# Casts of w_out for the second head group, moved behind units of the first products

## The chip, the cores and the metric

The kernel runs on one core of a Trainium2 chip. Its five engines work side by side, each from its own queue in order: TensorE (PE in the profile; its weight loads are PEld), VectorE (DVE), ScalarE (ACT), GpSimd (POOL), and SyncE (SP), which here only issues transfers. The metric is the time of one execution on the device in microseconds (us), lower is better; the median of the runs is compared.

## The reference

An encoder trunk of two layers on 1024 tokens of width 1024, in float32. Each layer computes

```
h = rmsnorm(x, g_pre_mix);  z = h @ w_in;  zf, zq, zk, zv, zm = split(z)
y_f = fourier_mix(zf, w_fourier)                 # 256 wide
y_a = window_attention(rope(zq), rope(zk), zv, sink)   # 8 query heads, 2 key heads, window 128: 512 wide
y_m = memory_attention(zm, keys and values of mem)     # 4 heads on 256 memory rows: 256 wide
y = concat(rmsnorm(y_f), rmsnorm(y_a), rmsnorm(y_m), each with its part of g_grp) @ w_out
x = x + rmsnorm(y, g_post_mix)
h = rmsnorm(x, g_pre_ffn);  gate, up = split(h @ w_ffn_in)
x = x + rmsnorm((silu(gate) * up) @ w_ffn_out, g_post_ffn)
```

The change is about `w_out`, of shape 1024 x 1024: its rows 0 to 255 meet y_f, rows 256 to 767 meet y_a, rows 768 to 1023 meet y_m.

## The kernel before

**Numbers in two parts.** Products of large matrices run in the format float32r. A value is written as a high part, rounded to float32r, and a low part, the rest; a product is then three products, high x high, high x low and low x high (class `Acc`). So each weight tile has to be prepared: ScalarE casts the high part, VectorE (sometimes GpSimd) subtracts it from the value for the low part. For `w_out` the cast also multiplies by the gain `g_grp` of its row (lines 949 and 950, in `load_wout`), where the raw rows come through a ring of three buffers, `raws` (line 948 loads).

**Storage.** Most tiles lie at fixed places of two large arrays, `arena_r` (float32r) and `arena_f` (float32), cut into slots of 256 columns; `Ring` hands out a few places in turn, and a tile may be overwritten once its readers are through. `raws` has slots 0, 2 and 4 of `arena_f`.

**The stage around the change.** Tokens come in 8 tiles of 128. `w_out`'s rows are numbered by blocks k of 128. The stage has these parts, in the order in which they are traced:

- Queries (`q`) and memory attention (`mem_units`), woven with each other, and `fm_load`, which prepares blocks 0, 1, 6 and 7 of `w_out` (Fourier and memory) in the large tiles called `big`.
- `att_units(0)`, the window attention of the first head group: 9 units, one a token tile with the values one unit behind the scores. A unit computes scores on TensorE (line 771), mask and maximum on VectorE (772), exp on ScalarE (784), normalising on GpSimd (795), transposes on TensorE (808), the two parts of the probabilities (162 and 163), and the products with the values (823).
- Woven with these, `fm_units`: 8 units, one for each token tile, that multiply the Fourier and memory columns by their blocks of `w_out`. The text calls them the first products. Each has two column halves; in each half a first group of six matmuls is copied and scaled by ScalarE (line 1006), a second is added by VectorE (1008), and the sum goes to the DRAM tile `pmd`. Preparing a unit's input squares the memory part (960), sums it with TensorE (963) and makes the scale on GpSimd (967).
- `out_load`, one more unit in this weave: it prepares blocks 2 to 5 of `w_out`, which the window attention needs, at slots 32 to 63 of `arena_r`. These are the rows "for the second head group": the products that read them (in `out`, tile name `mo`, with both operands in `arena_r`) run when the second head group of the attention is under way.
- `att_units(1)`, the second head group, with `out`, the residual, the next norm, and the first blocks of the feed-forward network.

**What sets the order.** `weave` merges streams of units by their relative places, which gives the order of tracing. The traced order is only a priority: a planner with its own clock for every engine then lays out each engine's queue, and an instruction that it holds ready may go ahead of others that were traced before it. Casts that only need a load can thus go far ahead of their traced place. `tc.issue_after(ins)` holds them back: what is traced inside it on the engine of `ins` stands behind `ins` in that engine's queue. It adds no wait for `ins` to finish. Transfers that SyncE issues stand in SyncE's queue in planned order; each waits there until the buffer that it writes is free.

In the weave before, the order was: attention unit 0, first products 0, attention 1, first products 1, and so on to attention 6, then `out_load` with all its loads and casts at once, attention 7, first products 6, attention 8, first products 7.

Of the kernel before, what the change touches and what calls it, by code (L numbers as in the profile page):

```python
# [15 lines left out]
AF = mybir.ActivationFunctionType  # L16
ALU = mybir.AluOpType
AX = mybir.AxisListType

P = 128  # L20
# [3 lines left out]
NK = D // P  # L24
# [34 lines left out]
def weave(*streams):  # L59

    order = []
    for si, units in enumerate(streams):
        order += [((i + 0.5) / len(units), si, i, u) for i, u in enumerate(units)]
    for *_, u in sorted(order, key=lambda o: o[:3]):
        u()
# [3 lines left out]
def tile_encoder(ctx: ExitStack, tc: tile.TileContext, T, C, out):  # L69
    nc = tc.nc  # L70
# [11 lines left out]
    def nm(s):  # L82
        uid[0] += 1
        return f"{s}_{uid[0]}"
# [18 lines left out]
    def shaped(ap, shape):  # L103
        names = "abcde"[: len(shape)]
        dims = {c: d for c, d in zip(names, shape)}
        return ap.rearrange(f"p ({' '.join(names)}) -> p {' '.join(names)}", **dims) if len(shape) > 1 else ap

    def at(k, *shape, dt=F32):

        t = arenas[F32R if dt is F32R else F32]  # L110
        if dt is not F32R and k >= 8:
            k, t = (k - 8, flex["t"]) if k < 16 else (k - 8, t)
        o = int(k * 256)
        ap = t[:, o : o + math.prod(shape)]
        return shaped(ap.bitcast(dt) if dt is I32 else ap, shape)

    def big(*shape, dt=F32R):

        return bp.tile([P, *shape], dt, tag="big", name=nm("big"))
# [12 lines left out]
    def run(k, n, step):  # L132
        return Ring(*[k + i * step for i in range(n)])


    raws, junks = run(0, 3, 2), Ring(56)
# [17 lines left out]
    def ps(shape, name="ps", tag="pd"):  # L154
        return psp[tag].tile([P] + list(shape), F32, tag=tag, name=nm(name))

    f32 = lambda ap: ap.bitcast(F32)
# [22 lines left out]
    def cst(*shape):  # L180
# [20 lines left out]
        out=mask[:, 0:P], in_=mask[:, 0:P], pattern=[[1, P]], compare_op=ALU.is_ge,  # L201
# [4 lines left out]
        out=mask[:, 2 * P : 3 * P], in_=mask[:, 2 * P : 3 * P], pattern=[[-1, P]],  # L206
# [3 lines left out]
    ggT = cst(DEPTH * NK)  # L210
# [285 lines left out]
    class Mix:  # L496
# [440 lines left out]

        def load_wout(self, ks, k0=None):

            w = [big(2, D) if k0 is None else at(k0 + 8 * j, 2, D, dt=F32R) for j in range(len(ks))]  # L940
            res = {k: (w[j][:, 0], w[j][:, 1]) for j, k in enumerate(ks)}
            for n in range(2):
                ns = slice(n * 512, n * 512 + 512)
                for k in ks:
                    hi, lo = res[k]
                    g = ggT[:, self.l * NK + k : self.l * NK + k + 1]
                    raw = raws(512)
                    nc.sync.dma_start(raw, T["w_out"][self.l, k * P : (k + 1) * P, ns])
                    nc.scalar.activation(hi[:, ns], raw, AF.Copy, scale=g)
                    nc.vector.scalar_tensor_tensor(  # L950
                        out=lo[:, ns], in0=raw, scalar=g, in1=f32(hi[:, ns]), op0=ALU.mult, op1=ALU.subtract
                    )
            return res

        def group_scale(self, parts, n, ring):

# [24 lines left out]
        def fm_units(self, pmd):  # L981

            st = {}

            def prep(t):
                half, c = divmod(t, 4)
                sl = slice(c * P, c * P + P)
                yf, ym = self.yf[half][:, :, sl], self.ym[half][:, :, sl]
                st[t] = self.split_y((yf, ym), yys), self.group_scale((ym,), MW, sqs)

            def unit(t):
                if t == 0:
                    prep(0)
                (hi, lo), rs = st.pop(t)
                for n in range(2):
                    ns = slice(n * 512, n * 512 + 512)
                    f = pms(512)
                    for gi in range(2):
                        pt = ps([512], "mo")
                        acc = Acc(pt, 2)  # L1000
                        for i in range(2):
                            j = 2 * (1 - gi) + i
                            w = self.wfm[(0, 1, 6, 7)[j]]
                            acc.add(hi[:, j], lo[:, j], w[0][:, ns], w[1][:, ns])
                        if gi == 0:
                            nc.scalar.activation(f, pt, AF.Copy, scale=rs[:, 0:1])
                        else:
                            nc.vector.tensor_tensor(out=f, in0=pt, in1=f, op=ALU.add)
                    nc.scalar.dma_start(pmd[t][:, ns], f)
                if t + 1 < NT:  # L1010
                    prep(t + 1)

            return [lambda t=t: unit(t) for t in range(NT)]

        def out_load(self):
            self.woa = self.load_wout((2, 3, 4, 5), 32)

        def out_gains(self):
            self.gpost = gain(T["g_post_mix"][self.l], at(48, D))
# [332 lines left out]
    mix = Mix(0, hT, mem)  # L1352
# [13 lines left out]
    for l in range(DEPTH):  # L1366
# [6 lines left out]
        mem.load()  # L1373
        weave(mix.mem_units(), q[1:8] + [mix.fm_load] + q[8:])
        fm = mix.fm_units(pmd)
        weave(mix.att_units(0), fm[:6] + [mix.out_load] + fm[6:])
        mix.out_gains()
        xs = x_in if l == 0 else x2d
        hb = Blocks()
# [45 lines left out]
        if l + 1 < DEPTH:  # L1425
            mem = Memory(l + 1, 16, 0, 16, 28, "pT")
            mix = Mix(l + 1, nhT, mem)
# [83 lines left out]
```

## Time and profile before

| | |
|---|---|
| median of 3 runs | 2069.59 us (2065.72 to 2076.48) |
| the profiled execution's own time | 2072.77 us |
| its span, first to last instruction | 2070.9 us |
| mean granted TensorE clock | 0.981 |
| busy: TensorE, VectorE, ScalarE, GpSimd | 2001.5, 1546.8, 1061.7, 714.1 us |
| the stage of the change, layer 0 and layer 1 | about 207 to 294 us and 1227 to 1319 us |

A row of the views of groups and of time has the engine, the line of the kernel, the operation, and output <- inputs by tile names. In brackets stands how long the engine sat idle before it, and what ended that. A row of the view by stage has, for each engine, the busy time in that window and the number of instructions, then the granted TensorE clock as a share of full speed, the share of the transfer engines, and their rate. A row of the waits has who waited, for whom, the total in us, how many times, and the longest.

### The profile page before, as it was taken

The page shows a single profiled execution, that of the slowest core. Times are in us where ns is not written, and L with a number is a line of the kernel's source. Part 1 is how long each engine was busy: PE and PEld are TensorE (multiplying, and loading weights), DVE is VectorE, ACT ScalarE, POOL GpSimd, SP SyncE. Part 2 cuts the span into 40 slices and gives each one's busy share as a digit, 9 for nine tenths or more (in the row PEclk, how much of TensorE's full clock was granted, in tenths as well). Part 3 has the DMA queues.
Part 4 walks back from the last instruction along what each step waited for, and adds up shares of the span by engine and source line. Part 5 has one row for each costly group of instructions (what it writes and reads, how often), then busy time and mean ns, then how long its engine had stood idle before and what let it go on. Part 6 is the DMA issues. An engine that isn't in the chain of part 4 may idle for free.

```text
span 2070.9 us, 28456 instructions
## 1 busy us (share of the span) xinstructions
PE 2001.5 (97%) x9587; PEld 1638.0 (79%) x9587; DVE 1546.8 (75%) x2496; ACT 1061.7 (51%) x2250; POOL 714.1 (34%) x819
## 2 busy tenths in 40 slices
PE   7999999899999999999999989997999999999998
PEld 6877777678888888887888768775888888878886
DVE  5556767888787786768876776579887787778767
ACT  6466777643333333455545677775433333345542
POOL 4354445433343333002423544363342342320002
PEclk9999999899999999999999999998999999999999
DMA  6110222423233233879841122233332233269974
GB/s 212 48 57 31 103 97 102 143 77 107 89 120 97 97 112 104 297 266 332 281 175 39 57 67 93 83 123 121 97 126 95 87 132 97 97 217 342 305 257 155
DMA packets 173634, 286.47 MB, mean 138 GB/s; under 512 B 15496, under 2 KB 73392, under 8 KB 173488
## 3 DMA queue, kind: packets, MB, share of 16 engines
q1 hardware_dynamic: 165424, 265.78, 38.7%
q10 hardware_dynamic: 8064, 18.88, 2.4%
q8 instruction: 75, 1.23, 0.2%
q14 instruction: 71, 0.58, 0.1%
HBM read 218.02 MB, written 66.58 MB: 137 GB/s over the span
## 4 chain that ended last, share of the span: by engine, by line
PE 85%; DVE 4%; DMA 3%; ACT 3%; POOL 3%; issue 2%; SPq 0%; DVEq 0%; POOLq 0%; ACTq 0%
PE fo L1277 19%; PE qz L1142 12%; PE qx L1142 11%; PE qy L1142 11%; PE mo L173 7%; PE qw L1142 6%; PE kvp L173 4%; PE qp L173 4%; PE zT L173 2%; PE pT L808 2%; PE sc L771 1%; DVE arena_r L163 1%; PE av L823 1%; PE av L816 1%; PE mav L916 1%
## 5 line engine op out<-in xcount | busy, mean ns | idle before, releaser
L162 ACT CAST arena_r<-arena_f 128x512 fp32r<-128x512 f32 (+2 forms) x714 | 411.5, 598 | 631.1 <-PE qz L1142 119.8
L163 DVE TENSOR_TENSOR arena_r<-arena_f,arena_r 128x512 fp32r<-128x512 f32 x632 | 476.5, 775 | 138.0 <-ACT arena_r L162 129.7
L1277 PE MATMUL fo<-arena_r 128*128 128x512 f32 x1848 | 424.7, 391 | 5.8 <-ACT arena_r L162 5.8
L1277 PEld LDWEIGHTS fo<-arena_r 128*128 128x128 f32 x1848 | 347.0, 188 | 78.8 <-ACT arena_r L162 4.4
L1142 PE MATMUL qy<-arena_r 128*128 128x512 f32 x1056 | 263.7, 400 | 16.5 <-ACT arena_r L162 11.1
L1142 PEld LDWEIGHTS qy<-arena_r 128*128 128x128 f32 x1056 | 203.3, 193 | 62.6 <-ACT arena_r L162 11.8
L1132 DVE TENSOR_TENSOR arena_f<-arena_f 128x512 f32<-128x512 f32 x220 | 201.9, 924 | 11.5 <-DMA arena_f<-in_w_ffn_in 5.0
L1142 PE MATMUL qz<-arena_r 128*128 128x512 f32 x704 | 199.1, 395 | 2.5 <-ACT arena_r L162 1.9
L1162 POOL TENSOR_TENSOR arena_f<-arena_f 128x512 f32<-128x512 f32 x44 | 71.8, 1633 | 313.7 <-ACT arena_f L1147 313.7
L1142 PEld LDWEIGHTS qz<-arena_r 128*128 128x128 f32 x704 | 134.2, 191 | 31.9 <-ACT arena_r L162 2.6
L1142 PE MATMUL qx<-arena_r 128*128 128x512 f32 x528 | 127.9, 390 | 0.4 <-ACT arena_r L162 0.4
L1142 PE MATMUL qw<-arena_r 128*128 128x512 f32 x528 | 127.3, 389 | 0.0
L1142 PE MATMUL qx<-big,arena_r 128*128 128x512 f32 x528 | 126.8, 389 | 0.0
L1142 PEld LDWEIGHTS qx<-arena_r 128*128 128x128 f32 x528 | 99.2, 188 | 21.7 <-ACT arena_r L162 1.2
L1142 PEld LDWEIGHTS qx<-big,arena_r 128*128 128x128 f32 x528 | 99.1, 188 | 20.6
L1142 PEld LDWEIGHTS qw<-arena_r 128*128 128x128 f32 x528 | 99.1, 188 | 20.6
L1142 PE MATMUL qz<-big,arena_r 128*128 128x512 f32 x352 | 115.2, 389 | 0.0
L221 POOL TENSOR_SCALAR rrsv<-rss 128x1 f32<-128x1 f32 x32 | 17.7, 554 | 259.3 <-ACT arena_f L334 207.3
L173 PE MATMUL qp<-big,arena_r 128*128 128x512 f32 x384 | 99.5, 404 | 2.0 <-POOL big L163 2.0
L173 PE MATMUL mo<-big,arena_r 128*128 128x512 f32 x384 | 101.4, 400 | 0.0
L1194 POOL TENSOR_TENSOR arena_f<-arena_f,flex 128x512 f32<-128x512 f32 x32 | 52.5, 1640 | 139.7 <-DVE arena_f L1174 101.0
L173 PE MATMUL mo<-arena_r 128*128 128x512 f32 x384 | 100.2, 401 | 0.3 <-POOL arena_r L163 0.3
(245 smaller groups left out, 3532.8 us busy)
## 6 DMA issues: line engine op xcount, KB each, us to landing
arena_f<-in_w_ffn_out SPq DMA_DIRECT2D x264, 256.0 KB, 4.6
arena_f<-in_w_ffn_in SPq DMA_DIRECT2D x88, 512.0 KB, 3.6
actd<-arena_f SPq DMA_DIRECT2D x154, 256.0 KB, 3.7
arena_f<-actd SPq DMA_DIRECT2D x154, 256.0 KB, 4.6
arena_f<-in_w_in SPq DMA_DIRECT2D x40, 256.0 KB, 2.8
arena_f<-in_x SPq DMA_DIRECT2D x16, 512.0 KB, 4.8
arena_f<-in_w_out SPq DMA_DIRECT2D x32, 256.0 KB, 2.7
pmd<-arena_f ACTq DMA_DIRECT2D x32, 256.0 KB, 2.0
```

The source lines that it names most:

```text
L162: nc.scalar.copy(hi, src)
L163: return (lo_eng or nc.vector).tensor_tensor(out=lo, in0=src, in1=f32(hi), op=ALU.subtract)
L173: mm(self.dst, a, b, start=self.i == 0, stop=self.i == self.n - 1)
L771: mm(pt, lhs, self.kst[g][i][:, k0 * P : k1 * P], start=i == 0, stop=i == 1)
L808: nc.tensor.transpose(pT[:, h, :], es_[h // 2][:, h % 2, j * P : j * P + P], ident)
L816: mm(av[64 * s : 64 * s + 64, 0 : 2 * P], self.v32[:, k0 + j], rhs, start=j == 0, stop=j == nk - 1)
L823: mm(av, lhs, p_, start=j == 0 and i == 0, stop=j == nk - 1 and i == 1)
L1132: nc.vector.tensor_tensor(out=s, in0=a, in1=b, op=op)
L1142: mm(pt, a, b, start=start and n == 0, stop=n == 11, skip_group_check=not start)
L1162: nc.gpsimd.tensor_tensor(out=self.v, in0=self.v, in1=self.s2, op=ALU.add)
L1194: (G if i in (0, 3) else V).tensor_tensor(out=a[i], in0=c, in1=g[i], op=ALU.mult)
L1277: mm(pt, ab[:, 0, x, sl], ab[:, 1, y], start=new and first and j == 0, stop=last and j == 2, skip_group_check=not new)
```

## The change

`load_wout` is split: `wout_units` returns its eight pieces of work (column half by block, each one load, one cast, one low part) as units, and `load_wout` calls them at once, as before, for blocks 0, 1, 6 and 7. For blocks 2 to 5 the eight units are put into the weave two by two, and each of their casts is traced inside `issue_after` on the last scaled copy (line 1006) traced so far.

```
         def wout_units(self, ks, k0=None, behind=None):
...
+            def unit(n, k):
                 ns = slice(n * 512, n * 512 + 512)
...
+                raw = raws(512)
+                nc.sync.dma_start(raw, T["w_out"][self.l, k * P : (k + 1) * P, ns])
+                with tc.issue_after(self.scaled.ins) if behind else ExitStack():
                     nc.scalar.activation(hi[:, ns], raw, AF.Copy, scale=g)
+                nc.vector.scalar_tensor_tensor(
+                    out=lo[:, ns], in0=raw, scalar=g, in1=f32(hi[:, ns]), op0=ALU.mult, op1=ALU.subtract
+                )
+
+            return res, [lambda n=n, k=k: unit(n, k) for n in range(2) for k in ks]
...
-                            nc.scalar.activation(f, pt, AF.Copy, scale=rs[:, 0:1])
+                            self.scaled = nc.scalar.activation(f, pt, AF.Copy, scale=rs[:, 0:1])
...
         def out_load(self):
-            self.woa = self.load_wout((2, 3, 4, 5), 32)
+            self.woa, units = self.wout_units((2, 3, 4, 5), 32, True)
+            return units
...
-        weave(mix.att_units(0), fm[:6] + [mix.out_load] + fm[6:])
+        ld = mix.out_load()
+        weave(mix.att_units(0), fm[:2] + [u for i in range(4) for u in ld[2 * i : 2 * i + 2] + fm[2 + i : 3 + i]] + fm[6:])
```

The second stream of the weave has 16 pieces now instead of 9, so the first products' places among the attention units change too. The traced order is, with A for an attention unit, F for a unit of the first products and W for a piece of `w_out`, all counted from 0: F0 A0 F1 W0 A1 W1 A2 F2 W2 A3 W3 F3 A4 W4 W5 A5 F4 W6 A6 W7 A7 F5 F6 A8 F7. W0 and W1 are pinned behind F1's second scaled copy, W2 and W3 behind F2's, W4 and W5 behind F3's, W6 and W7 behind F4's. The low parts on VectorE and the loads on SyncE are not pinned. The data, the number of instructions and the places in memory are the same.

More of the change, by code (lines that the diff above doesn't have):

```diff
@@ L938, in load_wout, with wout_units @@
         def load_wout(self, ks, k0=None):
+            res, units = self.wout_units(ks, k0)
+            for u in units:
+                u()
+            return res
+        def wout_units(self, ks, k0=None, behind=None):
             w = [big(2, D) if k0 is None else at(k0 + 8 * j, 2, D, dt=F32R) for j in range(len(ks))]
             res = {k: (w[j][:, 0], w[j][:, 1]) for j, k in enumerate(ks)}
-            for n in range(2):
+            def unit(n, k):
                 ns = slice(n * 512, n * 512 + 512)
[L944 to L948, printed above, removed]
+                hi, lo = res[k]
+                g = ggT[:, self.l * NK + k : self.l * NK + k + 1]
+                raw = raws(512)
+                nc.sync.dma_start(raw, T["w_out"][self.l, k * P : (k + 1) * P, ns])
+                with tc.issue_after(self.scaled.ins) if behind else ExitStack():
                     nc.scalar.activation(hi[:, ns], raw, AF.Copy, scale=g)
[L950 to L953, printed above, removed]
+                nc.vector.scalar_tensor_tensor(
+                    out=lo[:, ns], in0=raw, scalar=g, in1=f32(hi[:, ns]), op0=ALU.mult, op1=ALU.subtract
+                )
+            return res, [lambda n=n, k=k: unit(n, k) for n in range(2) for k in ks]
         def group_scale(self, parts, n, ring):
```

## The prediction

> **What bounds the kernel now.** I read the page first, then the busy times by stage around the moved casts, then who TensorE waited for in those stages, and then the queues of ScalarE and VectorE in order of time.
>
> From the page:
>
> ```profile
> span 2070.9 us, 28456 instructions
> PE 2001.5 (97%) x9587; PEld 1638.0 (79%) x9587; DVE 1546.8 (75%) x2496; ACT 1061.7 (51%) x2250; POOL 714.1 (34%) x819
> ```
>
> TensorE is the bound: 2070.9 - 2001.5 = 69.4 us of its span are idle, over the whole kernel. A change that moves casts can take only some of that, or add to it.
>
> The moved casts are line 949 with an arena_r output, 8 in each layer, each followed by its low part, line 950, on VectorE. The instructions of line 949 (x, ns min/median/max, first and last start):
>
> ```profile
> L949 ACT ACTIVATE arena_r<-arena_f,const x16: 707/722/755, 207.9 to 1243.3; 128x512 fp32r<-128x512 f32 x16
> ```
>
> All 16 lie in two stretches, which I call the heads of the stage. The next view gives busy time for each head and then for the rest of its stage, in layer 0 and layer 1, and for a window at the end.
>
> ```profile
> core 0: us, PE busy (x) PEld busy (x) DVE busy (x) ACT busy (x) POOL busy (x), PEclk, DMA share, GB/s
> 207.00:226.00 19.00, 15.74 (x76) 9.74 (x75) 15.64 (x49) 16.96 (x45) 8.08 (x15) 1.00 0.35 114
> 226.00:294.00 68.00, 68.00 (x364) 57.57 (x365) 43.74 (x129) 47.03 (x121) 27.94 (x48) 1.00 0.31 106
> 1227.00:1245.00 18.00, 14.52 (x79) 9.25 (x77) 16.63 (x46) 17.12 (x47) 10.51 (x18) 1.00 0.34 111
> 1245.00:1319.00 74.00, 74.00 (x396) 62.05 (x393) 49.57 (x154) 52.40 (x141) 29.94 (x52) 1.00 0.30 102
> ```
>
> ```profile
> 300.00:310.00 10.00, 9.00 (x55) 6.16 (x53) 6.09 (x27) 10.00 (x32) 5.49 (x10) 1.00 0.00 0
> ```
>
> In the heads TensorE is idle 19 - 15.74 = 3.26 us and 18 - 14.52 = 3.48 us, together 6.74 us, while ScalarE is busy 0.89 and 0.95 of the time and VectorE 0.82 and 0.92. In the rest of the stage TensorE has no idle time that the view shows, and ScalarE is at 47.03/68 = 0.69 and 52.40/74 = 0.71. So the casts sit where ScalarE and VectorE bind, and go to where TensorE binds. That is the case for the change; its size is what the 6.74 us allow.
>
> What TensorE waited for in the two heads (total us, times, longest):
>
> ```profile
> PE mav L916 <- ACT arena_f L908: 1.7, 2, 1.4
> PE sc L771 <- DVE rmax L772: 0.8, 3, 0.3
> PE pT L808 <- POOL arena_f L795: 0.4, 1, 0.4
> ```
>
> ```profile
> PE mpT L906 <- POOL arena_f L896: 1.7, 3, 0.8
> PE sc L771 <- DVE rmax L772: 1.2, 2, 0.8
> PE mav L916 <- ACT arena_f L908: 0.5, 1, 0.5
> ```
>
> No row names a cast: line 949 delays what TensorE waits for only by standing in front of it in an engine's queue. ScalarE's queue in order of time (start, us):
>
> ```profile
> 207.90 0.72 ACT L949 ACTIVATE arena_r<-arena_f,const 128x512 fp32r<-128x512 f32 x1
> 208.53 0.40 ACT L960 ACTIVATE arena_f<-arena_f 128x256 f32<-128x256 f32 x1
> 208.83 1.05 ACT L908 COPY arena_f<-mpT 128x512 f32<-128x512 f32 x2
> ...
> 217.02 0.72 ACT L949 ACTIVATE arena_r<-arena_f,const 128x512 fp32r<-128x512 f32 x1 [1.13 <-DMA arena_f<-in_w_out]
> 217.65 0.49 ACT L784 ACTIVATE arena_f<-arena_f,nmx 128x256 f32<-128x256 f32 x1
> ...
> 1227.30 0.72 ACT L949 ACTIVATE arena_r<-arena_f,const 128x512 fp32r<-128x512 f32 x1
> 1227.91 0.57 ACT L417 CAST arena_r<-qT 64x512 fp32r<-64x512 f32 x1
> 1228.38 1.07 ACT L908 COPY arena_f<-mpT 128x512 f32<-128x512 f32 x2
> ```
>
> And VectorE's:
>
> ```profile
> 213.15 1.05 DVE L950 SCALAR_TENSOR_TENSOR arena_r<-arena_f,const,arena_r 128x512 fp32r<-128x512 f32 x1
> 214.13 0.41 DVE L772 CUSTOM_DVE_ANT_0 arena_f<-sc,const 128x256 f32<-128x256 f32 x1
> ...
> 216.27 0.15 DVE L778 SCALAR_TENSOR_TENSOR nmx<-rmax,const 128x4 f32<-128x4 f32 x1
> ...
> 1235.30 0.75 DVE L950 SCALAR_TENSOR_TENSOR arena_r<-arena_f,const,arena_r 128x512 fp32r<-128x512 f32 x1
> 1235.97 0.42 DVE L772 CUSTOM_DVE_ANT_0 arena_f<-sc,const 128x256 f32<-128x256 f32 x1
> ```
>
> One cast holds ScalarE for 208.53 - 207.90 = 0.63 us, one low part holds VectorE for 1235.97 - 1235.30 = 0.67. The worst is at 217.02: the cast waits 1.13 us for its own load, and the exps (line 784) stand behind it although their bias was ready at 216.27 + 0.15 = 216.42. They start 217.65 - 216.42 = 1.23 us late.
>
> **The change part by part.** No instruction is added or removed: 8 loads, 8 casts and 8 low parts in each layer, as before. Moved are: the casts (pinned), the low parts (behind their casts), the loads from the fourth on (three raw buffers), and the traced places of the first products' units among the attention units.
>
> Taken from the heads. A wait can lose at most the one cast in front of it.
> - 1.4 us before mav, layer 0: the cast at 207.90 delays line 908 by 0.63. Gain 0.63.
> - 0.4 before pT, layer 0: its probabilities come from the exps that were 1.23 late. Gain 0.4.
> - sc, layer 0, 0.8 in three: the low part at 213.15 holds the mask and maximum (line 772) for 0.98 us; one wait, 0.3.
> - mav, layer 1, 0.5: the cast at 1227.30. Gain 0.5, all of it.
> - sc, layer 1, the longest of 0.8: the low part at 1235.30. Gain 0.67.
> - mpT, layer 1, 1.7 in three: this chain goes through VectorE, where a low part can cost between 0 and 0.67; I take 0.3.
>
> Sum 0.63 + 0.4 + 0.3 + 0.5 + 0.67 + 0.3 = 2.8 us. The bounds are 0 (each wait's next releaser is as late) and 6.74 (all idle time of the heads).
>
> Added behind the first products. 16 casts at 0.63 are 10.1 us of ScalarE, 5 us in each layer; its share there becomes (47.03 + 5.0)/68 = 0.77 and (52.40 + 5.0)/74 = 0.78. 16 low parts at 0.67 make VectorE (43.74 + 5.4)/68 = 0.72. What hides them is TensorE's own queue, which has no idle time in either window. If that cover were gone, every cast would show: 10.1 us, the upper bound; below nothing it cannot go, as nothing there waits on these casts. I take the end near 0, 0.5 us, since with ScalarE at 0.69 to 0.71 TensorE's idle time is nothing.
>
> Is the last cast early enough? It goes behind the fifth unit's second scaled copy, the tenth line 1006 of the layer; the first reader is the second head group's product:
>
> ```profile
> 263.80 0.69 ACT L1006 ACTIVATE arena_f<-mo,grs 128x512 f32<-128x512 f32 x1
> ...
> 1287.37 0.69 ACT L1006 ACTIVATE arena_f<-mo,grs 128x512 f32<-128x512 f32 x1
> ```
>
> ```profile
> L173 PE MATMUL mo<-arena_r x384: 387/393/501, 293.9 to 1407.1; 128*128 128x512 f32 x192
> ```
>
> ```profile
> 1319.03 1.55 PE L173 MATMUL mo<-arena_r 128*128 128x512 f32 x6
> ```
>
> 293.9 - 263.8 = 30 us and 1319.0 - 1287.4 = 32 us of cover. Cost 0; if it were gone, the output product of the first token tile would wait, and TensorE has only attention to fill with.
>
> The loads. A fourth load can go out when the first low part has read its buffer, a unit ahead of its cast (eight units in 68 us, so 8.5 us); it lands in
>
> ```profile
> DMA to landing us min/median/max: 2.5/2.7/3.8
> ```
>
> so no cast should wait. On SyncE's queue these loads now pass, or are passed by, the early loads of the residual stage; one of those (the projected rows of tile 2) goes into raw buffers 0 and 2 and must now wait for the last casts. It is read long after 300 us. Cost 0. The same holds for POOL's sum of the values (line 834), which overwrites the third raw buffer and is read only from the second head group on.
>
> [...] At 213.15 the low part took 1.05 instead of 0.75 while this ran:
>
> ```profile
> 211.82 1.85 POOL L896 TENSOR_SCALAR arena_f<-arena_f,rden 128x256 f32<-128x256 f32 x4 [4.30 <-DVE rden L894]
> ```
>
> [...]
>
> **The sum.** The profiled execution took 2072.77 us, its span 2070.9 and 1.9 around it. 2072.77 - 2.8 + 0.5 = 2070.5. The median of the runs is 2069.59, 3.2 below this execution; on that scale 2069.59 - 2.3 = 2067.3, so **2067**.
>
> **Rivals.**
>
> 1. The heads clear completely. Units 0 and 1 of the first products are now traced ahead of attention units 0 and 1, so the planner may also fill the heads with them. All 6.74 us go: 2063. For: ScalarE and VectorE are the only thing late there. Against: the remaining waits run through chains of three engines (maximum, exp, normalising, transposes) that the casts do not lengthen. A larger form: weight loads take only 9.74/19 = 0.51 and 9.25/18 = 0.51 of the heads, against 57.57/68 = 0.85 in the rest. Were 0.85 possible, the heads would need (9.74 + 9.25)/0.85 = 22.3 us instead of 37: 14.7 us of room, 2055. Against that form:
>
> ```profile
> 209.45 1.07 PE L916 MATMUL mav<-arena_f 128*64 128x512 f32 x2 [1.43 <-ACT arena_f L908]
> ```
>
> Two products of the memory values take 1.07 us here, so few loads belong to much of the work. [...]
>
> 2. Nothing to see: the big tiles' casts and the softmax chains keep the heads as late as they are. Casts hidden before, hidden after: 2069.6.
>
> 3. Slower: the end of the stage. Of the 16 traced pieces, units 4 and 5 of the first products now come later among the attention units (4 behind attention unit 5 instead of 4, 5 behind 7 instead of 5, all counted from 0), so more of the first products falls into 300 to 310 us, where ScalarE is at 10.00 of 10. A unit brings two scaled copies of 0.69 and about three instructions of line 960's size (0.40): 2.6 us. Up to two units in each layer make 10.4 us: 2080; it is slower than before from the point where one unit falls there, since 2 x 2.6 is more than the 2.8 gained. For: the full window. Against: TensorE is idle there for only 1 us, and more first products there would also fill it.
>
> 4. Slower: a moved load stands on SyncE's queue behind a load that waits for something else, its cast then holds ScalarE with the exps behind it, as at 217.02. One landing of 2.7 for each of three pairs in two layers is 16 us: 2086. Against: the loads have a unit's time in hand.
>
> **How the numbers follow.** I give the forecast 0.46, rival 2 0.15, rival 1 at 2063 0.13 and in the direction of 2055 0.08, rival 3 0.12, rival 4 0.06. Faster or slower means by over 0.5%, about what a measurement of this kernel can tell: below 2059.2 or above 2079.9. Faster: 0.08 and some of 2063, with the runs' own spread (2065.72 to 2076.48), 0.13. Slower: rival 4 and about half of rival 3, 0.12. Within: 0.75. The range takes in rival 1 at 2063 with the spread below it and rival 3 at its price: 2057 to 2079. The likeliest case's own range is 2062 to 2072.
>
> **What would show it.** Right: no line 949 with arena_r output before the second unit's scaled copies (line 1006); ScalarE below 0.8 in the head; mav's wait of 1.4 us near 0.8; TensorE still without idle time to 290 us. Wrong: idle TensorE between 226 and 310 us released by line 949, 784 or 162 (rival 3 if it lies behind 290), or line 949 waiting for a load of w_out (rival 4). A difference that arises after 390 us, at the start of the feed-forward network, would be a new order by the planner that none of these steps holds.

## The result and the profile after

| | before | after |
|---|---|---|
| median (12 runs each) | 2071.40 us (2065.72 to 2076.58) | 2066.66 us (2061.78 to 2072.07) |
| profiled execution's own time | 2072.77 us | 2072.07 us |
| its span, granted clock | 2070.9 us, 0.981 | 2070.3 us, 0.986 |

The ratio of after to before is 0.9969, with an interval of [0.9955, 0.9983]: faster by 0.3%, which is some 6 us (the medians of the table lie 4.7 us apart), and within 0.5%. The forecast was 2.3 us. The profiled execution of after is the slowest of its 12; a second profile of the same kernel (run e1 below) had a span of 2059.0 us, so where the two disagree both are shown.

From the page of after:

```profile
PE 1994.9 (96%) x9587; PEld 1634.8 (79%) x9587; DVE 1551.5 (75%) x2496; ACT 1059.5 (51%) x2250; POOL 715.3 (35%) x819
```

TensorE is busy 2001.5 - 1994.9 = 6.6 us less with the same 9587 matmul instructions, at a higher mean clock. That is the first sign that the gain isn't idle time taken out.

**The casts went where the change sends them.** The group of the moved casts in after (line 957 there; the scaled copy they are pinned behind is line 1015), and ScalarE's queue around the first pair:

```profile
L957 ACT ACTIVATE arena_r<-arena_f,const x16: 708/711/714, 229.8 to 1282.3; 128x512 fp32r<-128x512 f32 x16
```

```profile
229.20 0.68 ACT L1015 ACTIVATE arena_f<-mo,grs 128x512 f32<-128x512 f32 x1
229.78 1.32 ACT L957 ACTIVATE arena_r<-arena_f,const 128x512 fp32r<-128x512 f32 x2
```

The pair stands right behind a scaled copy, without the 1.13 us in which a cast of before waited for its load.

**The stage by busy time.** The same parts of the stage in after (head, rest of the first products, products of the second head group, for each layer):

```profile
202.00:221.00 19.00, 17.63 (x96) 12.09 (x94) 13.92 (x51) 15.73 (x48) 9.08 (x19) 1.00 0.13 45
221.00:292.00 71.00, 69.39 (x369) 58.80 (x368) 51.76 (x152) 53.62 (x138) 30.87 (x49) 1.00 0.37 123
292.00:381.00 89.00, 87.49 (x514) 67.33 (x513) 61.88 (x125) 64.10 (x161) 48.80 (x76) 1.00 0.34 116
1223.00:1241.00 18.00, 16.24 (x85) 9.95 (x84) 12.27 (x40) 15.12 (x49) 8.25 (x17) 1.00 0.14 45
1241.00:1319.00 78.00, 76.14 (x409) 64.43 (x408) 59.58 (x176) 60.44 (x163) 34.75 (x57) 1.00 0.33 112
1319.00:1407.00 88.00, 86.57 (x501) 65.66 (x500) 60.40 (x120) 59.17 (x150) 45.65 (x72) 1.00 0.33 117
```

And the two parts of before that the prediction didn't show:

```profile
294.00:390.00 96.00, 93.24 (x538) 70.13 (x536) 68.36 (x150) 69.87 (x182) 51.75 (x80) 1.00 0.33 114
1319.00:1407.00 88.00, 87.80 (x519) 68.14 (x518) 60.23 (x131) 65.89 (x170) 46.61 (x77) 1.00 0.33 113
```

TensorE's idle time (window less busy), both layers together:

| part | before | after |
|---|---|---|
| heads | 6.74 us | 1.37 + 1.76 = 3.13 us |
| rest of the first products | 0 | 1.61 + 1.86 = 3.47 us |
| second head group | 2.76 + 0.20 = 2.96 us | 1.51 + 1.43 = 2.94 us |
| sum | 9.70 us | 9.54 us |

The heads are relieved by 3.6 us, and 3.5 us of new idle time stand behind the first products. The runs e2 and e3 below tell apart what the moved casts and the new order of the units did here. TensorE's waits there in after, layer 0 from 221 us and layer 1 from 1241 us:

```profile
PE mo L173 <- DVE flex L845: 1.1, 1, 1.1
PE sc L771 <- DVE rmax L772: 0.4, 1, 0.4
```

```profile
PE av L823 <- DVE arena_r L163: 1.5, 1, 1.5
```

These waits all name VectorE, which also makes the moved low parts. The stage as a whole has not less idle time than it had.

**The start of the feed-forward network.** The gain is found behind the stage. The first 60 us after the last product of `out`, layer 0, first of before, then of after, in steps of 10 us:

```profile
390.00:400.00 10.00, 3.44 (x12) 2.28 (x12) 9.56 (x16) 5.34 (x10) 4.04 (x4) 0.62 0.35 121
400.00:410.00 10.00, 9.32 (x23) 6.83 (x24) 9.28 (x14) 4.66 (x9) 3.35 (x2) 0.53 0.33 103
410.00:420.00 10.00, 6.98 (x33) 5.11 (x31) 9.17 (x15) 5.92 (x12) 2.94 (x2) 0.98 0.30 106
420.00:430.00 10.00, 8.54 (x19) 5.81 (x20) 10.00 (x18) 5.38 (x11) 0.00 (x0) 0.51 0.01 2
```

```profile
381.00:391.00 10.00, 3.99 (x15) 2.65 (x14) 9.21 (x14) 5.42 (x11) 7.34 (x5) 0.67 0.39 125
391.00:401.00 10.00, 6.96 (x23) 5.21 (x23) 9.19 (x14) 5.69 (x10) 3.12 (x3) 0.84 0.61 191
401.00:411.00 10.00, 7.14 (x33) 5.08 (x32) 9.96 (x16) 5.76 (x11) 0.00 (x0) 0.97 0.18 52
411.00:421.00 10.00, 10.00 (x45) 8.02 (x44) 8.81 (x16) 7.00 (x14) 4.95 (x2) 1.00 0.01 2
```

The first three rows of both are nearly alike in matmul instructions started (12, 23, 33 and 15, 23, 33; products and transposes together, in the text "products"). In the fourth, before starts 19 at a granted clock of 0.51, and after 45 at 1.00: that is the difference. What TensorE had in its queue there, first before (its fourth row begins at 420 us; the last line shown are the next 22 `qz` products), then after:

```profile
413.54 3.02 PE L1142 MATMUL qy<-arena_r 128*128 128x512 f32 x12 [0.68 <-ACT arena_f L1147]
416.40 0.60 PE L1071 MATMUL hTp<-const,arena_f 128*128 128x128 f32 x4
418.12 0.66 PE L1071 MATMUL hTp<-const,arena_f 128*128 128x128 f32 x4 [1.12 <-ACT big L1072]
420.49 1.22 PE L1142 MATMUL qz<-arena_r 128*128 128x512 f32 x2 [1.71 <-ACT arena_r L162]
423.90 8.10 PE L1142 MATMUL qz<-arena_r 128*128 128x512 f32 x22 [0.54 <-DVE arena_r L163]
```

```profile
402.28 0.63 PE L1081 MATMUL hTp<-const,arena_f 128*128 128x128 f32 x4 [0.64 <-DVE arena_f L305]
403.39 2.57 PE L1152 MATMUL qy<-arena_r 128*128 128x512 f32 x10 [0.48 <-DVE arena_r L163]
405.81 0.60 PE L1081 MATMUL hTp<-const,arena_f 128*128 128x128 f32 x4
408.14 3.01 PE L1152 MATMUL qy<-arena_r 128*128 128x512 f32 x12 [1.74 <-ACT arena_f L1157]
```

`hTp` are the transposes of the normalised tokens (two halves of four for the last tile), `qy` and `qz` the first products of the feed-forward network. In before all 48 `qy` products of the tiles that are ready stand ahead of the last tile's transposes, and behind these nothing is left to do but wait for their copies and casts. In after the planner set the transposes behind 26 and 36 of the 48, so that 22 `qy` products fill the gaps. The change touches none of these instructions; their places are the planner's.

### The profile page after: what moved, and what is told of

It is laid out like the page before. It is cut to its first block, busy times and chain, and to the rows that moved or that the text cites. A ratio compares the mean times of both kernels' runs of the same rounds, so it can differ in the third digit from the quotient of the medians.

```text
span 2070.3 us, 28479 instructions
## 1 busy us (share of the span) xinstructions
PE 1994.9 (96%) x9587; PEld 1634.8 (79%) x9587; DVE 1551.5 (75%) x2496; ACT 1059.5 (51%) x2250; POOL 715.3 (35%) x819
## 4 chain that ended last, share of the span: by engine, by line
PE 79%; DVE 5%; DMA 5%; POOL 4%; ACT 4%; issue 3%; SPq 0%; DVEq 0%; POOLq 0%; ACTq 0%
PE fo L1287 16%; PE qz L1152 11%; PE qx L1152 11%; PE qy L1152 11%; PE mo L173 6%; PE qw L1152 5%; PE qp L173 4%; PE kvp L173 4%; PE zT L173 2%; DVE arena_r L163 2%; PE pT L808 1%; PE sc L771 1%; DMA arena_f<-in_w_ffn_out 1%; DMA arena_f<-actd 1%; POOL arena_f L795 1%
## 5 line engine op out<-in xcount | busy, mean ns | idle before, releaser
L1287 PE MATMUL fo<-arena_r 128*128 128x512 f32 x1848 | 429.1, 394 | 13.0 <-ACT arena_r L162 10.9
L1152 PE MATMUL qz<-arena_r 128*128 128x512 f32 x704 | 195.5, 389 | 0.0
L163 POOL TENSOR_TENSOR arena_r<-arena_f,arena_r 128x256 fp32r<-128x256 f32 (+2 forms) x82 | 68.1, 835 | 97.0 <-ACT arena_r L162 72.8
```

The lines of the kernel that those rows point to most:

```text
L163: return (lo_eng or nc.vector).tensor_tensor(out=lo, in0=src, in1=f32(hi), op=ALU.subtract)
L1152: mm(pt, a, b, start=start and n == 0, stop=n == 11, skip_group_check=not start)
L1287: mm(pt, ab[:, 0, x, sl], ab[:, 1, y], start=new and first and j == 0, stop=last and j == 2, skip_group_check=not new)
```

## The experiments

In the expectations, H is the prediction's reading (the heads of the stage carry the gain, the new place costs next to nothing), and S the theory formed on the comparison above: the gain arises at the start of the feed-forward network, from how many `qy` products stand ahead of the last transposes.

To read all runs alike, each execution is cut at the same instructions: "stage" runs from the first product of the memory scores (`ms`; in layer 1 from the last product of the queries, `qp`) to the last product of `out` (`mo`), and "start" from there to the last `qy`. For layer 0 of after, they come from these rows (first and last start):

```profile
L884 PE MATMUL ms<-flex,arena_r x64: 274/282/385, 138.6 to 201.2; 128*128 128x256 f32 x64
L173 PE MATMUL mo<-arena_r x192: 387/393/504, 295.6 to 381.4; 128*128 128x512 f32 x192
L1152 PE MATMUL qy<-arena_r x528: 387/389/796, 387.8 to 810.8; 128*128 128x512 f32 x176
```

The stage is 381.4 - 138.6 = 242.8 us and the start 810.8 - 381.4 = 429.4 us. "Ahead" is the number of `qy` products ahead of each half of the last transposes (one number where both halves stand together), layer 0 then layer 1; "products" is the number of matmul instructions, transposes among them, that TensorE began in the first 60 us after the last `mo`.

| run | ratio to before [interval] | ahead | products | stage 0 | start 0 | stage 1 | start 1 | sum |
|---|---|---|---|---|---|---|---|---|
| before | 1 | 48; 26 | 172; 199 | 247.6 | 435.9 | 192.4 | 431.8 | 1307.7 |
| e9, before again | 1.0007 [0.9991, 1.0024] | 48; 26 | 172; 207 | 250.5 | 435.8 | 192.6 | 429.8 | 1308.7 |
| after | 0.9969 [0.9955, 0.9983] | 26/36; 26/36 | 200; 206 | 242.8 | 429.4 | 196.0 | 430.1 | 1298.3 |
| e1, after again | 0.9951 [0.9933, 0.9969] | 26/36; 26/36 | 202; 204 | 242.8 | 428.9 | 195.8 | 430.5 | 1298.0 |
| e2, pin only | 0.9940 [0.9920, 0.9961] | 26; 26 | 208; 212 | 246.0 | 427.6 | 195.2 | 427.2 | 1296.0 |
| e11, pin only again | 0.9937 [0.9919, 0.9955] | 26; 26 | 197; 213 | 242.0 | 430.1 | 193.6 | 427.0 | 1292.7 |
| e3, order only | 0.9981 [0.9966, 0.9997] | 36/48; 26 | 189; 220 | 245.2 | 431.7 | 202.5 | 426.9 | 1306.3 |
| e4, no casts | 1.0023 [1.0009, 1.0037] | 48; 48 | 171; 171 | 246.5 | 436.1 | 195.5 | 436.1 | 1314.2 |
| e5, before, transposes early | 1.0020 [1.0007, 1.0034] | 24; 24 | 194; 192 | 240.2 | 431.7 | 202.6 | 431.3 | 1305.8 |
| e6, after, transposes late | 1.0017 [1.0004, 1.0029] | 48; 48 | 174; 188 | 245.2 | 435.3 | 195.9 | 434.3 | 1310.7 |
| e7, casts twice | 1.0011 [0.9995, 1.0026] | 36/48; 26 | 179; 206 | 245.2 | 434.0 | 201.1 | 429.9 | 1310.2 |
| e8, pin only, transposes early | 1.0001 [0.9986, 1.0016] | 24; 24 | 196; 195 | 240.2 | 431.2 | 198.3 | 432.7 | 1302.4 |
| e10, before, 12 products held | 0.9981 [0.9967, 0.9995] | 36; 26 | 192; 204 | 250.5 | 431.2 | 193.3 | 430.4 | 1305.4 |

Two profiles of one kernel agree within 0.6 us in the start of layer 0 (e2 and e11: 2.5 us), 2.0 us in the start of layer 1, and 3 to 4 us in the stage of layer 0. Smaller differences than these are not read from the lengths. For all runs but e5 and e8, whose stage begins some 5 to 11 us later than the others', the sums go with the ratios to within 4 us. All starts with 48 products ahead of both halves took 434.3 to 436.1 us, and all others 426.9 to 434.0. Among these the number doesn't order them: with 26 ahead they took 426.9 to 431.8 us.

**The stage without the clock's part.** Most of what one kernel's stage varies by is the granted clock. In some executions it is at half for a stretch of the stage, in others of the same queues it is not, as at the stage's start in e9 (after and e1 have 1.00 there):

```profile
138.00:145.00 7.00, 6.14 (x18) 5.14 (x19) 6.84 (x13) 3.96 (x8) 4.50 (x6) 0.51 0.02 4
```

As an estimate from the clock of 0.51, half of TensorE's busy time in such stretches is lost, here 6.14/2 = 3.1 us, and 4.7 in the whole stage with a second such stretch at 353 us (0.98 over the window from 291 to 388 us). The next table takes that off each stage. Beside it stands TensorE's idle time in two parts, both layers together: A from the first of the first products (`mo` from `big`) to the first `mo` of the second head group (the heads and what follows them), B from there to the last `mo`. For before, A is 91.00 - 87.74 us of the window from 202.9 to 293.9 us and 97.70 - 93.18 us of the one from 1221.3 to 1319.0.

| run | stage 0 less the loss | stage 1 less the loss | sum | idle A | idle B |
|---|---|---|---|---|---|
| before; e9 | 246.0; 245.8 | 192.4; 192.6 | 438.4; 438.4 | 7.8; 8.1 | 3.0; 2.8 |
| after; e1 | 242.8; 242.8 | 196.0; 195.8 | 438.8; 438.6 | 7.4; 7.6 | 2.9; 3.0 |
| e2; e11 (pin only) | 241.2; 242.0 | 193.6; 193.6 | 434.8; 435.6 | 4.5; 4.5 | 4.1; 4.0 |
| e3 (order only) | 243.5 | 196.0 | 439.5 | 9.4 | 2.5 |
| e4 (no casts) | 243.4 | 195.5 | 438.9 | 5.2 | 5.0 |
| e7 (casts twice) | 243.6 | 201.1 | 444.7 | 9.0 | 4.1 |

By this measure two profiles of one kernel agree within 0.8 us. (e6 and e10 have the stage's queues of after and of before; e5 and e8 are left out, as their queues differ from the start on.) The change took some 3 us from stage 0 and added as much to stage 1.

**e1, the changed kernel again** (no edit), for a second profile of it.

> The changed kernel once more, for a second profile. In the first profile of it the heads' idle TensorE fell from 6.7 us to 3.1, but 3.5 us of idle time appeared behind the first products, and the feed-forward start of layer 0 ran at a granted clock of 0.98 instead of 0.80. Theory H (the heads): ratio 0.997, and the place of the gain is the time from the first product mo to the last one, shorter by 2 to 4 us in each layer. Theory S (the start of the feed-forward network, where the planner's order of the last transposes has moved): ratio 0.997 too, but the stage as long as before and 6 us won between the last mo and the last qy of layer 0. If the clock of 0.98 was chance, this profile shows about 0.80 there.

Ratio 0.9951, and all four parts within 0.5 us of after's. Against the mean of before and e9, e1 has 249.1 - 242.8 = 6.3 us less in stage 0 (that part alone varies by 3 us), 3.3 us more in stage 1, 6.9 us less in start 0, and 0.3 us less in start 1. The two stages together are 3.0 us shorter, but without the clock's part they are as long as before (438.6 against 438.4), so this is chance; start 0 is the part that stands clear of it.

**e2 and e11, the pin without the new order.** The traced order of attention units and first products is that of before; only the casts move. The weave, against that of before (the pin itself is the change's):

```
-        weave(mix.att_units(0), fm[:6] + [mix.out_load] + fm[6:])
+        ld = mix.out_load()
+        pair = [lambda i=i: [u() for u in (fm[i], ld[2 * i - 2], ld[2 * i - 1])] for i in range(1, 5)]
+        weave(mix.att_units(0), fm[:1] + pair + [fm[5], lambda: None] + fm[6:])
```

> The casts are pinned two by two behind the same units as in the change, but attention units and first products keep the traced order of before. Theory H: all of the gain is here, 0.996 to 0.998. Theory S (the new weave order and what the planner makes of the feed-forward start): 1.000, with the feed-forward start of layer 0 between. Either: no cast with an arena_r output in the heads.

> The kernel that only pins, once more, as the candidate to beat both: 0.994 to 0.996 by its first timing. Theory S: 428 and 427 us from the last mo to the last qy, as in its first profile.

0.9940 and 0.9937: at least as fast as the whole change, and the fastest version of the study (median 2059.96 us in e11). So the new traced order isn't needed for the gain. Its starts took 854.8 and 857.1 us (before 867.7, 865.6). Its stages took 441.2 and 435.6 us (before 440.0, 443.1); without the clock's part that is some 3 to 4 us less than before. TensorE in the head of layer 0, behind it, and the same in layer 1, up to the second head group, in e2:

```profile
205.00:224.00 19.00, 17.28 (x88) 11.97 (x87) 13.53 (x49) 14.00 (x40) 9.06 (x18) 1.00 0.19 60
224.00:290.80 66.80, 66.64 (x360) 56.69 (x359) 49.74 (x138) 52.44 (x137) 26.74 (x43) 1.00 0.38 127
1220.00:1238.00 18.00, 16.20 (x81) 9.94 (x81) 12.56 (x40) 14.85 (x47) 7.42 (x16) 1.00 0.15 47
1238.00:1313.70 75.70, 75.62 (x415) 64.25 (x414) 56.79 (x172) 58.39 (x153) 32.11 (x52) 1.00 0.35 115
```

The heads' idle time is 1.72 + 1.80 = 3.5 us, as in after, but behind the first products it is 0.16 + 0.08 = 0.24 us, although the 16 casts stand there too and ScalarE is at 0.79 and 0.77. With the second head group (1 us more than before) the stage has 8.6 us of idle time (8.5 in e11), 2.2 to 2.4 less than the 10.8 and 10.9 of before and e9. That is the reading H, and nearly the forecast's own size, but for the pin without the new order.

**e3, the new order without the pin.** The weave of after, with `wout_units((2, 3, 4, 5), 32)`, so that no cast is held back.

> The eight units in the new weave order, but nothing pinned: the planner puts the casts into the heads as before. Theory H: no gain, 1.000, with ScalarE at 0.9 and 3 us of idle TensorE in each head. Theory S: the gain is here, 0.997, with the last transposes of the stage among the first qy products as in the changed kernel.

0.9981. The two stages took 447.7 us, 9.1 more than e1's 438.6. Most of that is no price of the casts' place: in the head of layer 1 this one profile had half the clock,

```profile
1227.00:1241.00 14.00, 13.39 (x47) 10.78 (x46) 9.38 (x32) 11.53 (x34) 8.00 (x12) 0.51 0.21 73
```

and without the clock's part the stages are 439.5 against 438.6 us. In idle time A the pin is worth 1.8 to 2.0 us in the new order (9.4 to 7.4 and 7.6) and 3.3 to 3.6 in the old (7.8 and 8.1 to 4.5). The new order by itself adds 1.3 to 1.6 us (7.8 and 8.1 to 9.4), and does not relieve the heads. The starts are 7 to 9 us shorter than before's (two profiles).

**e4, no casts at all.** Before, with the 16 loads, casts and low parts of blocks 2 to 5 left out; the products read whatever lies at those slots.

```
-            self.woa = self.load_wout((2, 3, 4, 5), 32)
+            w = [at(32 + 8 * j, 2, D, dt=F32R) for j in range(4)]
+            self.woa = {2 + j: (w[j][:, 0], w[j][:, 1]) for j in range(4)}
```

> Traced order of before, with the 16 loads, casts and low parts of blocks 2 to 5 of w_out left out (the products then read what is left in those slots, so the output is not the reference's). This is the most that any place for the casts can give. Theory H: 0.995 to 0.997, since the heads are relieved and nothing is added later; by the forecast 2.8 us in the heads, 6.7 at most. Theory S: 1.000 or any small difference that the order of the feed-forward start makes, whose PE order is that of before here.

Slower, 1.0023, with less work. The two heads, by busy time in e4:

```profile
204.00:223.00 19.00, 16.66 (x86) 11.07 (x86) 11.90 (x44) 13.02 (x39) 9.14 (x18) 1.00 0.04 15
1222.00:1240.00 18.00, 15.34 (x86) 10.43 (x85) 14.69 (x41) 15.94 (x49) 9.27 (x18) 1.00 0.05 18
```

TensorE is still idle 2.34 + 2.66 = 5.0 us there: without any cast only 1.7 of the 6.74 us go. By idle time A, which doesn't depend on where a head's window is cut, it is 2.6 to 2.9 us, of which 2.0 to 2.2 come back in B. The stages together took 442.0 us, between before's 440.0 and 443.1. Here the planner laid out the stage anew without the casts, and nothing of the relief is left in its length; the time lost is at the start of layer 1, where all 48 products now stand ahead of the transposes as in layer 0 (431.8 to 436.1 us).

**e7, the price of the new place.** After, with each of the 16 pinned casts and its low part made twice.

```
+                for _ in range(2 if behind else 1):
+                    with tc.issue_after(self.scaled.ins) if behind else ExitStack():
+                        nc.scalar.activation(hi[:, ns], raw, AF.Copy, scale=g)
+                    nc.vector.scalar_tensor_tensor(
+                        out=lo[:, ns], in0=raw, scalar=g, in1=f32(hi[:, ns]), op0=ALU.mult, op1=ALU.subtract
+                    )
```

> The changed kernel with each of the 16 moved casts and its low part made twice, at the new place. The forecast's price of the new place was 0.5 us for 16 casts: by it this differs from the changed kernel by under 1 us in the stretch from the first mo to the last mo. If every cast shows there, that stretch is 5 us longer in each layer. The start of the feed-forward network has 36 and 48 qy ahead of the last transposes in layer 0 and 26 in layer 1, so by theory S it adds 3 us in layer 0 and takes 3 in layer 1.

The stages took 2.4 and 5.3 us more than e1's, 7.7 us for 16 more casts with their low parts; without the clock's part it is some 6 us, 0.4 us each, of 0.63 on ScalarE and 0.67 on VectorE. This is a rough price from one profile, nearly all of it in layer 1, and TensorE's order in the stage is no longer that of after (from 234 us on), so it is not the casts' alone. It is the price of one more cast in the new order, where one stands already; the first 16 cost 0.24 us of idle time in the old order (e2). The other part of the slowdown is start 0 (434.0), where the order fell back to 36 and 48.

**e6, after with the last transposes late.** One edge that adds no wait: the last tile's transposes stand behind all 48 `qy` products, as in layer 0 of before. Up to the start of the feed-forward network all queues are those of after.

```
+                    lastqy[0] = mm(pt, a, b, start=start and n == 0, stop=n == 11, skip_group_check=not start)
...
+                with tc.issue_after(lastqy[0].ins) if i == NT + 3 else ExitStack():
+                    hb.tile(hs.pop(i - 4), i - 4)
```

> The changed kernel, with the last tile's transposes held behind all 48 qy products on TensorE's queue in both layers, which is where the kernel before has them in layer 0. Theory S: the stretch from the last mo to the last qy rises from 429 us to about 436 in layer 0 and from 430 to about 436 in layer 1, the gain is gone: 0.999 to 1.002. Theory H: the heads stay relieved and the gain stays, 0.996.

1.0017: the whole gain is gone, and more. Start 0 took 435.3 us, 5.9 more than after's and 0.6 less than before's; start 1 434.3, 4.2 more than after's. In the first 60 us of start 0 its clock was between those of the two (0.86; before 0.77, after 0.91), and TensorE was idle 3 us longer than in either (14.9 us): here the late order cost idle time as well as clock.

**e10, before with 12 products held.** The other direction: in before, the first of the last 12 `qy` products gets an edge without a wait that puts it behind the last transposes. All queues of layer 0 are those of before until there.

```
+                if i == NT + 3:
+                    tc.add_manual_dep(
+                        held[0].ins, lastT[0].ins.name,
+                        mybir.DependencyInfo(mybir.DependencyClass.NoSync, mybir.DependencyReason.DATA),
+                        reason="held",
+                    )
```

> The kernel before with one edge more: in TensorE's queue the up half's product 4 stands behind the last token tile's transposes. All queues are those of before up to the start of layer 0's feed-forward network; there 36 qy products stand ahead of the last transposes instead of 48, and VectorE's queue follows. Layer 1 has 26 already and keeps them. Casts are where they were. Theory S: the stretch from the last mo to the last qy of layer 0 falls from 436 us to about 432, as in the run with the new order only, nothing else moves: 0.998. Theory H: 1.000.

0.9981 [0.9967, 0.9995], with start 0 at 431.2 us, 4.7 less than before, and stage 0 at 250.5 as in e9. TensorE's queue in e10:

```profile
417.36 0.63 PE L1071 MATMUL hTp<-const,arena_f 128*128 128x128 f32 x4 [2.42 <-DVE arena_f L305]
418.67 1.11 PE L1071 MATMUL hTp<-const,arena_f 128*128 128x128 f32 x4 [0.68 <-ACT big L1072]
419.43 4.10 PE L1143 MATMUL qy<-arena_r 128*128 128x512 f32 x12
424.28 5.15 PE L1143 MATMUL qz<-arena_r 128*128 128x512 f32 x22
```

The 12 products stand where before had its waits, and the 22 `qz` products then take 5.15 us, where the 22 of before at 423.90 took 8.10. This is the cleanest test of S: the stage has its old casts and its old order, and a good part of the gain of the change is there.

**e5 and e8, the transposes earlier by the traced order.** Two groups of 12 `qy` products (`uq`, the up half, with their load) are traced one step later, behind the last tile's transposes, in before (e5) and in the pin-only version (e8), so that 24 `qy` products stand ahead of the transposes.

```
+            if i == NT + 3:
```

> The kernel before, casts untouched, with one edit elsewhere: at the start of the feed-forward network the up half's products 2 and 4 are traced behind the last token tile's transposes. On TensorE's queue 24 qy products then stand ahead of the last transposes in both layers, instead of 48 in layer 0 and 26 in layer 1. Theory S (the place of the last tile's chain in the queues sets the start): the stretch from the last mo to the last qy falls in layer 0 from 436 us to about 427, and in layer 1 from 432 by 2 to 5; ratio 0.994 to 0.996, about the whole gain of the change without moving a cast. Theory H (the heads): 1.000, since the heads are as before.

> Casts pinned with the unit order of before, as in the run that pinned only, and the up half's products 2 and 4 traced behind the last transposes, as in the run that moved them alone. Theory S: 24 qy ahead of the last transposes in both layers where the pinned kernel has 26, so about the same as that: 0.993 to 0.995. If the two edits' gains added up, as theory H and S side by side would have it, 0.990.

Both missed: 1.0020 and 1.0001. The 24 came out in both layers of both runs, and the starts took 431.2 to 432.7 us: better than with 48, but not the 427 that was expected of fewer ahead. And the new traced order made the planner lay out every queue anew from the very start of the kernel (TensorE's differs within the first 15 us): the stage began at 147.0 and 148.6 us instead of 142.1, and stage 1 of e5 took 202.6. They change too much to test one thing by their whole time; e10 with its single edge does that.

**e9, before again** (no edit), for a second profile.

> The kernel before once more, for a second profile of it: ratio 1.000. If its first profile was a usual one, the last mo to the last qy takes 436 us in layer 0 and 432 in layer 1, and the two stages 248 us (first memory score to last mo, layer 0) and 192 us (last query product to last mo, layer 1). Its first memory score came 3.5 us later than in the kernels with pinned casts, whose queues are the same up to there; if that was chance it comes at 139 us here.

1.0007, an interval that holds 1. Start 0 is 435.8 us and 172 products again, so the slow start is a property of the order, not of one execution. It also shows how much stage 0 varies with the same queues (247.6 and 250.5, nearly all of it the clock's part), and that the 3.5 us by which after entered the stage earlier (138.6 against 142.1) are chance: e9 entered it at 137.5.

## Why the prediction was right, and where it was wrong

The time was right by its number: forecast 2.3 us faster, measured 0.3% (some 6 us), and "within 0.5%" held. For the change as it was made this is luck: the stage that was to carry the gain carried none of it, and what came arose elsewhere. The mechanism, casts out of the heads, was right for the pin without the new order (e2 and e11: 2.2 to 2.4 us of idle time less in the stage). The step that failed is the new order of the units. The sum has terms for the casts alone and puts the order at nothing; it appears only among the rivals. It costs TensorE some 3 us of idle time up to the second head group and some 2 in the whole stage, and all but some 0.4 us of the relief is gone with that (10.3 and 10.6 us in after and e1, 8.6 and 8.5 in e2 and e11).

- "Taken from the heads", 2.8 us: measured 3.6 (6.74 to 3.13). TensorE's waits in the heads of after, layer 0 and layer 1:

```profile
PE mav L916 <- ACT arena_f L908: 1.0, 2, 0.6
PE mpT L906 <- POOL arena_f L896: 0.2, 1, 0.2
```

```profile
PE mpT L906 <- POOL arena_f L896: 1.2, 2, 0.8
PE sc L771 <- DVE rmax L772: 0.3, 1, 0.3
PE mav L916 <- ACT arena_f L908: 0.2, 1, 0.2
```

  mav's longest in layer 0 went from 1.4 us to 0.6 (forecast near 0.8), sc's total in layer 1 from 1.2 to 0.3 and mav's from 0.5 to 0.2. The pin does this without the new order too (e2: 6.74 to 3.5), so it can be put down to the casts' place. What rival 1 named, units 0 and 1 of the first products traced ahead of the attention's, doesn't do it: with the new order alone (e3) idle time A is 9.4 us, where before and e9 have 7.8 and 8.1. That the heads don't clear is shown by e4, which leaves 5.0 us there with no cast at all.
- "Added behind the first products", 0.5 us for 16 casts: for the casts by themselves this came out well (e2: 0.24 us, with ScalarE at 0.79 and 0.77). In the change it was 3.47 us, at shares no higher, 53.62/71 = 0.76 and 51.76/71 = 0.73 in layer 0 (forecast 0.77 and 0.72). So it was not the share of ScalarE that set it, and the sign "TensorE still without idle time to 290 us" failed. What differs between after and e2 is the order of attention units and first products. The part A of e3 shows that the order costs 1.3 to 1.6 us without pinned casts; after against e2, with them, 2.9 to 3.1. Which of the units' places does it is not shown; the two longest waits, 1.1 and 1.5 us, were for VectorE. In mean the low parts of the moved casts took 0.85 us there, 0.78 in before and e2.
- So the two terms cancel in idle time (9.70 to 9.54 us), and in the stages' length without the clock's part (438.4 to 438.6 and 438.8).
- "Is the last cast early enough?" Yes: the last pinned cast starts at 1282.3 us, and the first product of the second head group in layer 1 at 1321.9.
- The loads cost nothing, as forecast. The moved casts of after, with the idle time of ScalarE before them as the last number:

```profile
L957 ACT ACTIVATE arena_r<-arena_f,const 128x512 fp32r<-128x512 f32 x16 | 10.6, 711 | 0.0
```

  No moved cast waited for its load, which removes rival 4.
- Rival 3 (end of the stage) saw that a later place of the units can cost time, but put it behind 300 us: the rows of the second head group show the same idle time as before, 2.94 against 2.96 us. It falls.
- Rival 2 (heads as late as before) falls by the heads, though its outcome for the stage, nothing, is what was seen.
- The prediction's last sentence named "a difference that arises after 390 us, at the start of the feed-forward network" as "a new order by the planner that none of these steps holds". That is what came, 6.7 us in layer 0 (mean of two profiles each: 435.85 to 429.15). It was named as a sign, and got neither a price nor a chance.

**What was shown of the cause.** The same stretch, 60 us from the last product of `out` in layer 0, in before, after, e6 and e10, in this order:

```profile
390.00:450.00 60.00, 48.28 (x172) 36.55 (x172) 55.06 (x81) 32.01 (x56) 17.99 (x12) 0.77 0.19 64
```

```profile
381.00:441.00 60.00, 48.09 (x200) 37.55 (x199) 57.13 (x84) 33.16 (x59) 22.27 (x13) 0.91 0.24 77
```

```profile
385.00:445.00 60.00, 45.13 (x174) 34.68 (x174) 54.25 (x79) 32.55 (x57) 19.23 (x13) 0.86 0.20 69
```

```profile
392.00:452.00 60.00, 49.68 (x192) 39.17 (x192) 56.77 (x85) 33.36 (x59) 22.52 (x13) 0.83 0.21 71
```

At full speed a product takes 10/45 of a microsecond here, about 0.22 (row 411 to 421 us of after). After starts 28 products more than before in these 60 us: 28 x 0.22 = 6.2 us, against 6.5 measured between them in start 0. For e10 it is 20 x 0.22 = 4.4 us against 4.7, and for e6 2 x 0.22 = 0.4 against 0.6. In all 13 profiles and both layers, the start plus 0.22 us for each product begun in its first 60 us comes to between 473.3 and 475.7 us: to within some 2 us, what tells these starts apart (426.9 to 436.1) is lost in the first 60 us. With e6 and e10, which move only what stands ahead of what and carry the time with them in both directions, it is shown that the order at this place is worth some 4 to 6 us in a layer (4.7 in e10, 5.9 and 4.2 in e6). That the change moved it there is the planner's doing; why it came out so is open, and by the table the edits upstream draw several such orders (48, 36/48, 26/36, 26).

What stays open too: why the clock is at half in the stage of some executions and not of others; why the stage of layer 1 took 3 us more at full clock in after and e4 (196 against 192.5 us); and whether the pin-only version (0.9937 and 0.9940) beats the whole change (0.9951 and 0.9969). Its starts of layer 1 (427.1 against 430.3 us) and its stages without the clock's part (435 against 439) point that way, but the intervals of the ratios overlap.

## What to carry to other kernels

When an edit does two things, price both: here the pin alone freed 2.2 to 2.4 us of TensorE's idle time in the stage, and the new order of units that came with it gave most of that back. A share of busy time on an engine doesn't say what an addition costs there: with ScalarE at 0.76 to 0.79 the same 16 casts went with 0.24 us of idle TensorE in one order and 3.47 in another. In a kernel whose queues a planner lays out, a local edit can also re-draw the order at a later place where an engine changes from scarce to plenty of work, so compare the traces there before putting a small gain down to the edit, look at the granted clock before comparing lengths, and hold the good order with an explicit edge if it matters. At such a place, count the instructions that the bound engine begins in a fixed time, not its busy share (here 172 and 200 in 60 us, at 48.28 and 48.09 us busy and granted clocks of 0.77 and 0.91).

## What the runs showed of the hardware

What was not expected is that between before and after the gain of layer 0 is one of clock, with no change in idle time. In the 60 us rows above, TensorE is busy 48.28 us in before and 48.09 in after, so it is idle the same 12 us; but the granted clock is 0.77 in the one and 0.91 in the other, and (0.91 - 0.77) x 48 = 6.7 us is the whole difference. That is not so in every run: e6 has a clock of 0.86 and 14.9 us of idle time, and is as slow as before. The second profiles, e9 for before and e1 for after, have the same clocks:

```profile
388.00:448.00 60.00, 48.27 (x172) 36.38 (x171) 55.09 (x81) 31.99 (x56) 17.76 (x12) 0.77 0.19 63
```

```profile
381.00:441.00 60.00, 48.57 (x202) 38.16 (x201) 57.58 (x85) 33.61 (x60) 20.38 (x13) 0.91 0.24 79
```

In before, waits of 0.68, 1.12 and 1.71 us lie between 412.9 and 420.5 us; the clock was 0.98 in the row to 420 and 0.51 in the row to 430. In that second row TensorE began 26 products fewer than after in its own, 5.7 us at full speed, though it was idle for only 1.46 us of it.

In the rows of 10 us the clock lies between 0.51 and 1.00. In before TensorE had no wait from 423.90 us on; in the 6.10 us from there to 430, all of them busy, the granted clock was still 0.51, and in the row from 430 to 440 it was 1.00. Whether the waits set the clock, and which of them, is not shown by these runs: after's queue has a wait of 1.74 us at 408.14, and the rows to 411 and to 421 us show 0.97 and 1.00.
